# A one-core diffusion step: Pool's low parts of weight blocks in pieces of 256 columns

## The chip, the cores and the metric

The program runs on one core of one Trainium2 chip. The metric is the device time of one execution in microseconds (us). The engines are named as in the profile: PE (matrix products), PEld (its weight loads, which overlap), DVE (VectorE), ACT (ScalarE), POOL (GpSimd) and SP (SyncE, which here issues the DMAs). A row with SPq is SP's queue.

## The reference

Two layers of a hybrid backbone in fp32, with shared weights for 128 context tokens and 1024 latent tokens, D_MODEL = 1024, D_FF = 2816:

```python
def layer(x, cond, w, ctx=None):
    ...
    mods = jax.nn.silu(cond) @ w_ada + b_ada
    ...
    h = rms_norm(x, g_pre_mix) * (1 + sc_m) + sh_m
    q_na, k_na, v_na, q_mla, ckv, k_rope, q_g, k_g, v_g = mixer_projections(
        h, w_in, mla_g_q, mla_w_uq, mla_g_kv, gqa_g_q, gqa_g_k)
    ...
    o = jnp.concatenate([o_na, o_mla, o_gqa], axis=-1) @ w_out
    x = x + gt_m * rms_norm(o, g_post_mix)
    h = rms_norm(x, g_pre_ffn) * (1 + sc_f) + sh_f
    x = x + gt_f * rms_norm(conv_ffn(h, ffn_w_up, ffn_conv_w, ffn_conv_b, ffn_w_down), g_post_ffn)
```

The three attentions are a neighbourhood attention, a multi-head latent attention and a grouped-query attention. `conv_ffn` is an up-projection, a convolution of width 3 over the tokens, a SiLU gate and a down-projection.

## The kernel before

The nine token tiles (128 tokens each, the context tile first) go through both layers together. A layer has five phases. The first is the projections with `w_in` (phase A), in layer 0 with the modulation's matrix `w_ada` among them. Then come the attentions. The output projection with `w_out` (phase C, `phase_c`) makes eight products of 1024 columns for each token tile, block k of the weights being row k of `w_out`; each tile ends with two RMS norms. The up-projection (`phase_u`) takes 44 blocks of `w_up` a layer, each with 72 matmuls of 384 columns (eight rows, three products, three groups of tokens), and DVE runs the convolution (L1020) behind them. The down-projection takes 66 loads of `w_down` a layer, in three groups of three token tiles, and ends each group with the norms of its tiles.

A matmul in fp32 is made of three products of rounded operands: high times high, high times low, low times high. So every operand is split. `load_w` (L341 to L350) brings 512 KB by one DMA of SP into one of two raw buffers (`wraw`, L348), and `split` (L194 to L200) makes two tiles from it: ACT copies the raw values into the rounded high part (L197), and Pool or DVE subtracts the high part from the raw one, which gives the low part (L200). Who subtracts is set by `lo_eng`: Pool for all of `w_up`; Pool and DVE in turn for `w_in`, `w_out` (even k on Pool, odd k on DVE) and `w_down`. The next DMA into a raw buffer waits until both parts were made from it. SP issues its DMAs in the order of the program, so what stands behind such a DMA waits with it: in the up-projection that is also `wadv` (L305), a piece of `w_ada` for `ada_dve`, in which DVE adds products of that piece into `aacc` (L308, L311) and PE then transposes the sums (L320).

In phase C DVE has one row of work at the start: the low parts of the nine tiles of `Y` (the attentions' output, last written at L734), named `hlo<-Y`, and of the odd weight blocks. The names of the weights' tiles there are `wu` for k = 0 and 1, `wd` for 2 and 3, `wx` for 4 to 7, so that the loads of the first four use the room of the FFN's weights. The products are in L973: for the first three token tiles k = 0 to 3 first, then the tiles one by one with the rest.

The norms run as `norm_tiles`: L166 multiplies the products in PSUM by the gain (`wt`), which frees PSUM for PE; `rsqrt_newton` makes 1/sqrt of a column in some six instructions of one column each (L116, L120, tiles `nw_t` and `nw_u`); L175 adds into the residual (`xt`). Each engine runs its instructions in the order in which the program issues them; the generators of several tiles are advanced in turn, so that one tile's Newton steps can stand ahead of another's L166 in DVE's row. The down-projection's products are L1125; the operand `g` is split like the weights.

Only blocks held as three-dimensional tiles are `weights` of 1024, 832 or 768 columns (a tile's two middle axes multiplied); those of 512 columns and two-dimensional tiles are split by the same function.

Of the kernel before, what the change touches and what calls it, by code (L numbers as in the profile page):

```python
# [14 lines left out]
F32 = mybir.dt.float32  # L15
# [4 lines left out]
ALU = mybir.AluOpType  # L20
# [25 lines left out]
def tile_kernel(ctx: ExitStack, tc: tile.TileContext, I, O):  # L46
    nc = tc.nc
    act, dve, pool, pe = nc.scalar, nc.vector, nc.gpsimd, nc.tensor
# [146 lines left out]
    def split(raw, hi, lo, hi_eng=None, lo_eng=None):  # L195
        if hi_eng is None:
            act.copy(hi, raw)  # L197
        else:
            hi_eng.tensor_copy(hi, raw)
        (lo_eng or pool).tensor_tensor(out=lo, in0=raw, in1=hi.bitcast(F32), op=ALU.subtract)  # L200

    def evac2(hi, lo, src, scale=None):

# [138 lines left out]
    def load_w(wp, src, tag, bufs, lo_eng=pool, wr=None):  # L342

        na, nb = src.shape[1:]
        raw = (wr or wp).tile([128, 1024], F32, name="wraw", bufs=2)
        out = [wp.tile([128, 1024], F32R, name=f"{tag}{i}", bufs=bufs) for i in range(2)]
        raw, hi, lo = [t.rearrange("p (a b) -> p a b", a=na)[:, :, :nb] for t in (raw, *out)]
        nc.sync.dma_start(out=raw, in_=src)  # L348
        split(raw, hi, lo, lo_eng=lo_eng)
        return hi, lo  # L350
# [12 lines left out]
    def phase_a(l, z, H, w, before, rest):  # L363
# [47 lines left out]
        ukv = [ml.tile([128, 512], F32R, name=f"ukv{i}", bufs=1) for i in range(2)]  # L411
        ckvT = [ml.tile([128, NT + 128], F32R, name=f"ckvT{i}", bufs=1) for i in range(2)]
        split(uq_r, uq[0], uq[1])
        split(ukv_r, ukv[0], ukv[1])
        split(cc_r, ckvT[0][:, 128:256], ckvT[1][:, 128:256])

# [809 lines left out]
    for l in range(L):  # L1226
# [49 lines left out]
        gens, xs, owner = [], {}, {}  # L1276
# [146 lines left out]
```

## Time and profile before

| | |
|---|---|
| time, median of 3 runs | 3352.62 us (3351.02 to 3357.26) |
| the profiled execution's own time | 3349.35 us |
| its span in the trace | 3347.5 us |
| PE busy | 3193.8 us, 95% of the span |
| DVE busy | 2164.2 us, 65% |
| ACT busy | 1545.5 us, 46% |
| POOL busy | 1127.4 us, 34%, 962 instructions |
| granted clock of PE, mean | 0.988 of full speed |

The profiled execution is one of many; its own time is measured around the program, the span is what the trace holds of it. Durations in the rows below come from that one execution. The busy share is an average: how much an engine's time is worth is read from the places where PE is idle. In the rows, the text in square brackets is the idle time of the engine just before the instruction, and what ended it.

### The profile page before, as it was taken

How to read it: one execution, taken by the hardware profiler on the slowest of the kernel's cores; microseconds unless marked ns; L12 is line 12 of the kernel's file. 1: busy time of each engine (PE TensorE's matmuls, PEld its weight loads, DVE VectorE, ACT ScalarE, POOL GpSimd, SP SyncE). 2: the span in 40 equal slices, each digit the busy share in tenths (PEclk: the TensorE clock that was granted, in tenths of full speed). 3: DMA queues.
4: the chain of work that ended last, by engine and by line, in shares of the span. 5: the costliest groups of instructions: out<-in, count | busy, mean ns of one | idle time of the engine just before them, and what ended most of it. 6: DMA issues, size and time to landing. Idle time of an engine off the chain costs nothing.

```text
span 3347.5 us, 50944 instructions
## 1 busy us (share of the span) xinstructions
PE 3193.8 (95%) x18068; PEld 2883.7 (86%) x18068; DVE 2164.2 (65%) x5367; ACT 1545.5 (46%) x3209; POOL 1127.4 (34%) x962
## 2 busy tenths in 40 slices
PE   8988999989999999999999899999899999999999
PEld 3868888877899999987788799888779999999887
DVE  5796788887787888435547728888768433333443
ACT  4321688885322222235544228888743222223443
POOL 2122345431233323344421314554313322323443
PEclk9999999999999999999999999999999999999999
DMA  7467431254244333255644563215523221213665
GB/s 244 137 180 225 138 78 46 62 158 144 85 142 127 118 120 118 79 186 192 194 139 135 152 194 84 54 46 128 167 87 107 88 73 60 73 66 122 205 205 167
DMA packets 224863, 428.77 MB, mean 128 GB/s; under 512 B 21089, under 2 KB 127457, under 8 KB 224609
## 3 DMA queue, kind: packets, MB, share of 16 engines
q1 hardware_dynamic: 223312, 424.33, 41.3%
q8 instruction: 143, 2.34, 0.3%
q10 hardware_dynamic: 1296, 1.19, 0.1%
q14 instruction: 112, 0.91, 0.1%
HBM read 324.05 MB, written 101.38 MB: 127 GB/s over the span
## 4 chain that ended last, share of the span: by engine, by line
PE 70%; DVE 14%; ACT 6%; issue 4%; DMA 3%; POOL 2%; SPq 1%; ACTq 0%; DVEq 0%; POOLq 0%
PE mm L1008 31%; PE mm L1125 15%; PE O L727 4%; PE T L709 4%; PE SA L679 3%; PE mm L973 3%; ACT P L689 2%; PE mm L591 2%; DVE PT L206 2%; ACT PT L205 2%; DVE aacc L311 2%; PE mm L376 1%; PE mm L375 1%; PE mm L374 1%; DVE nw_t L116 1%
## 5 line engine op out<-in xcount | busy, mean ns | idle before, releaser
L1008 PE MATMUL mm<-hhi,wu 128*128 128x384 f32 x4224 | 863.2, 335 | 2.4 <-POOL wu L200 1.5
L1008 PEld LDWEIGHTS mm<-hhi,wu 128*128 128x128 f32 x4224 | 742.6, 188 | 3.7 <-POOL wu L200 2.2
L1020 DVE SCALAR_TENSOR_TENSOR acc<-mm,conv,acc 128x336 f32<-128x336 f32 (+6 forms) x1408 | 412.6, 374 | 312.7 <-ACT acc L1045 312.5
L200 POOL TENSOR_TENSOR wu<-wraw,wu 128x1024 fp32r<-128x1024 f32 x123 | 301.9, 2456 | 688.5 <-ACT wu L197 673.8
L1008 PE MATMUL mm<-hlo,wu 128*128 128x384 f32 x2112 | 490.8, 334 | 0.0
L197 ACT CAST wu<-wraw 128x1024 fp32r<-128x1024 f32 x158 | 165.7, 1050 | 598.4 <-issue 371.8
L1008 PEld LDWEIGHTS mm<-hlo,wu 128*128 128x128 f32 x2112 | 377.1, 188 | 0.6 <-DVE hlo L153 0.4
L698 POOL TENSOR_SCALAR P<-P,rs 128x1152 f32<-128x1152 f32 (+3 forms) x288 | 273.3, 949 | 192.5 <-DVE rs L697 143.1
L727 PE MATMUL O<-PT,V 128*128 128x256 f32 (+1 forms) x1936 | 321.0, 295 | 10.8 <-DVE Y L734 10.8
L311 DVE SCALAR_TENSOR_TENSOR aacc<-wadv,sc,aacc 128x512 f32<-128x512 f32 x280 | 261.2, 976 | 65.6 <-DMA wadv<-w_ada 65.1
L709 PE MATMUL T<-ident,P 128*128 128x128 f32 x1736 | 282.4, 278 | 16.7 <-DVE PT L206 10.5
L679 PE MATMUL SA<-k,q 128*128 128x256 f32 (+5 forms) x1224 | 281.5, 350 | 11.5 <-DVE mx L818 3.8
L1125 PE MATMUL mm<-wd,g 128*128 128x512 f32 x1224 | 286.7, 390 | 2.6 <-DVE wt L166 2.6
L206 DVE TENSOR_TENSOR PT<-T,PT 128x512 fp32r<-128x512 f32 (+1 forms) x424 | 270.8, 646 | 22.2 <-ACT PT L205 16.7
L727 PEld LDWEIGHTS O<-PT,V 128*128 128x128 f32 x1936 | 258.3, 190 | 20.3 <-DVE Y L734 16.3
L1125 PE MATMUL mm<-wu,g 128*128 128x512 f32 x1152 | 272.1, 392 | 2.6 <-DVE wt L166 2.6
L1125 PEld LDWEIGHTS mm<-wd,g 128*128 128x128 f32 x1224 | 229.1, 188 | 51.0 <-DVE wt L166 3.5
L1125 PEld LDWEIGHTS mm<-wu,g 128*128 128x128 f32 x1152 | 217.2, 189 | 48.7 <-DVE wt L166 3.5
L205 ACT CAST PT<-T 128x512 fp32r<-128x512 f32 (+1 forms) x424 | 231.0, 561 | 53.3 <-PE T L709 39.0
L709 PEld LDWEIGHTS T<-ident,P 128*128 128x128 f32 x1736 | 199.6, 141 | 50.2 <-DVE PT L206 15.7
L679 PEld LDWEIGHTS SA<-k,q 128*128 128x128 f32 (+1 forms) x1224 | 197.9, 192 | 35.5 <-ACT P L689 7.2
L702 DVE TENSOR_REDUCE mx<-SA 128x1 f32<-128x896 f32 (+1 forms) x192 | 182.2, 949 | 33.2 <-PE SA L679 32.9
(207 smaller groups left out, 5083.0 us busy)
## 6 DMA issues: line engine op xcount, KB each, us to landing
wraw<-w_down SPq DMA_DIRECT2D x132, 512.0 KB, 3.6
wraw<-w_up SPq DMA_DIRECT2D x88, 512.0 KB, 3.6
wadv<-w_ada SPq DMA_DIRECT2D x160, 256.0 KB, 2.9
GT<-acc SPq DMA_DIRECT2D x44, 576.0 KB, 2.8
graw<-GT SPq DMA_DIRECT2D x132, 192.0 KB, 3.1
k<-KT SPq DMA_DIRECT2D x64, 320.0 KB, 5.9
q<-QT SPq DMA_DIRECT2D x48, 288.0 KB, 5.7
XD<-xt SPq DMA_DIRECT2D x27, 512.0 KB, 3.0
```

The costliest lines, as they stand in the source:

```text
L200: (lo_eng or pool).tensor_tensor(out=lo, in0=raw, in1=hi.bitcast(F32), op=ALU.subtract)
L205: act.copy(hi, src)
L206: dve.tensor_tensor(out=lo, in0=src, in1=hi.bitcast(F32), op=ALU.subtract)
L311: dve.scalar_tensor_tensor(out=accs[i], in0=w, scalar=sc[:, k, i:i + 1], in1=accs[i], op0=ALU.mult, op1=ALU.add)
L679: pe.matmul(out, q[0:rows, qc:qc + 128], kview(k[0:rows]), start=(i == 0), stop=(i == len(passes) - 1))
L698: pool.tensor_scalar(out=P[:, :n], in0=P[:, :n], scalar1=rs, scalar2=1.0, op0=ALU.mult, op1=ALU.mult)
L702: dve.tensor_reduce(out=out, in_=src, op=ALU.max, axis=AX.X, negate=True)
L709: pe.transpose(tp[:, j * 128:(j + 1) * 128], p, ident)
L727: pe.matmul(op[0][:, c0:c1], V[:, vt, :], PT[e][:, sl, c0:c1], start=(i == 0 and e == 0), stop=(i == last and e == 1))
L1008: pe.matmul(pts[c][:, :CN], a[:, k, :], h_[:, k, c * CN:(c + 1) * CN], start=(k == 0 and a is whi and h_ is hhi), stop=(k == KC - 1 and a ...
L1020: dve.scalar_tensor_tensor(out=d, in0=src, scalar=w, in1=d, op0=ALU.mult, op1=ALU.add)
L1125: pe.matmul(pts[j], a[:, ts], d[:, 0, j * 512:(j + 1) * 512], start=(f == 0 and n == 0), stop=(f == NFF - 1 and n == 2))
```

## The change

Pool's subtraction of a low part is cut into four instructions along the columns where the block is a three-dimensional tile of more than 512 columns. A block with eight rows of 128 columns (`w_up`, `w_down`) is cut into pairs of rows; one with a single row of 1024 (`w_out`) into four quarters of it; one with two rows (`w_in`, and the query's up-projection) into halves of each row. A piece has 256 columns (208 for the four blocks of 832, 192 for the two of 768). DVE's subtractions and ACT's copies stay whole.

```diff
-        (lo_eng or pool).tensor_tensor(out=lo, in0=raw, in1=hi.bitcast(F32), op=ALU.subtract)
+        for lo, raw, hi in quarters(lo, raw, hi) if lo_eng is None or lo_eng is pool else [(lo, raw, hi)]:
+            (lo_eng or pool).tensor_tensor(out=lo, in0=raw, in1=hi.bitcast(F32), op=ALU.subtract)
+
+    def quarters(*xs):
+
+        if len(xs[0].shape) != 3 or xs[0].shape[1] * xs[0].shape[2] <= 512:
+            return [xs]
+        na, nb = xs[0].shape[1:]
+        if na == 8:
+            return [[x[:, i:i + 2] for x in xs] for i in range(0, 8, 2)]
+        h = nb * na // 4
+        return [[x[:, a:a + 1, c:c + h] for x in xs] for a in range(na) for c in range(0, nb, h)]
```

It touches 178 blocks: 123 with the name `wu`, 37 `wd`, 4 `wx`, 12 `w` and 2 `uq`. They were 178 instructions and are now 712; nothing else is added, and no instruction passes another on any engine. In the program after, L200 stands at L201 and later lines 11 further down.

On Pool, at the start of phase C in layer 0, the row before (wu, wd, wx, wx are the low parts of blocks 0, 2, 4 and 6 of `w_out`):

```order
L698 TENSOR_SCALAR P<-P,rs 128x384 [waits DVE_49,PE_49]
L200 TENSOR_TENSOR wu_9418<-wraw,wu_9417 128x1024 [waits DMAHW4_49,DMAHW3_49,DMAHW5_49,DMAHW2_49,DMAHW6_49,DMAHW1_49,DMAHW7_49,DMAHW0_49,Activation_49]
L200 TENSOR_TENSOR wd_9434<-wraw,wd_9433 128x1024 [waits DMAHW4_49,Activation_49]
L200 TENSOR_TENSOR wx_9450<-wraw,wx_9449 128x1024 [waits DMAHW6_49,DMAHW7_49,DMAHW0_49,Activation_49]
L200 TENSOR_TENSOR wx_9466<-wraw,wx_9465 128x1024 [waits DMAHW1_49,DMAHW3_49,DMAHW0_49,DMAHW5_49,PE_49,Activation_49]
```

And the same place after:

```order
L709 TENSOR_SCALAR P<-P,rs 128x384 [waits DVE_49,PE_49]
L201 TENSOR_TENSOR wu_9439<-wraw,wu_9438 128x256 [waits DMAHW4_49,DMAHW3_49,DMAHW5_49,DMAHW2_49,DMAHW6_49,DMAHW1_49,DMAHW7_49,DMAHW0_49,Activation_49]
L201 TENSOR_TENSOR wu_9439<-wraw,wu_9438 128x256 x3
L201 TENSOR_TENSOR wd_9458<-wraw,wd_9457 128x256 [waits DMAHW4_49,Activation_49]
L201 TENSOR_TENSOR wd_9458<-wraw,wd_9457 128x256 x3
L201 TENSOR_TENSOR wx_9477<-wraw,wx_9476 128x256 [waits DMAHW6_49,DMAHW7_49,DMAHW0_49,Activation_49]
L201 TENSOR_TENSOR wx_9477<-wraw,wx_9476 128x256 x3
L201 TENSOR_TENSOR wx_9496<-wraw,wx_9495 128x256 [waits DMAHW1_49,DMAHW3_49,DMAHW0_49,DMAHW5_49,PE_49,Activation_49]
L201 TENSOR_TENSOR wx_9496<-wraw,wx_9495 128x256 x3
```

Every block stands where it stood, as four pieces, and the first piece has the waits of the whole one. The DMAs into the raw buffers on SP still wait for Pool's last piece.

On PE, in a block of the up-projection in layer 0 (wu_11027 and wu_11028 are the block's high and low part), the row before:

```order
L1008 MATMUL mm<-hhi,wu_11028 128x384 [waits Pool_49]
L1008 MATMUL mm<-hhi,wu_11028 128x384 x2
L1008 MATMUL mm<-hhi,wu_11027 128x384 x3
L1008 MATMUL mm<-hlo,wu_11027 128x384 x3
L1008 MATMUL mm<-hhi,wu_11028 128x384 x3
L1008 MATMUL mm<-hhi,wu_11027 128x384 x3
L1008 MATMUL mm<-hlo,wu_11027 128x384 x3
L1008 MATMUL mm<-hhi,wu_11028 128x384 x3
```

And after (wu_11072 and wu_11073 are the same two parts):

```order
L1019 MATMUL mm<-hhi,wu_11073 128x384 [waits Pool_49]
L1019 MATMUL mm<-hhi,wu_11073 128x384 x2
L1019 MATMUL mm<-hhi,wu_11072 128x384 x3
L1019 MATMUL mm<-hlo,wu_11072 128x384 x3
L1019 MATMUL mm<-hhi,wu_11073 128x384 x3
L1019 MATMUL mm<-hhi,wu_11072 128x384 x3
L1019 MATMUL mm<-hlo,wu_11072 128x384 x3
L1019 MATMUL mm<-hhi,wu_11073 128x384 [waits Pool_49]
L1019 MATMUL mm<-hhi,wu_11073 128x384 x2
```

Before, PE waited for Pool once a block; after, it waits again at every second of the eight rows, where the next piece begins.

## Rows read from the trace of the kernel before

**Rows 1.** The page's busy time, share of the span, instructions.

```profile
PE 3193.8 (95%) x18068; PEld 2883.7 (86%) x18068; DVE 2164.2 (65%) x5367; ACT 1545.5 (46%) x3209; POOL 1127.4 (34%) x962
```

**Rows 2.** Chain of waits, 1035 to 1080: start us, us, what.

```profile
1037.57 37.45 PE mm L1008 x216
```

**Rows 3.** Instructions of L200: duration ns min/median/max, first and last start us.

```profile
L200 POOL TENSOR_TENSOR wu<-wraw,wu x123: 2364/2405/3044, 740.8 to 3312.5; 128x1024 fp32r<-128x1024 f32 x123
L200 POOL TENSOR_TENSOR PT<-rt,PT x80: 727/735/746, 364.2 to 2296.6; 128x256 fp32r<-128x256 f32 x80
...
L200 DVE TENSOR_TENSOR hlo<-Y,hhi x18: 1209/1218/3365, 745.9 to 2406.1; 128x1024 fp32r<-128x1024 f32 x18
```

**Rows 4.** Instructions of L116, the Newton step.

```profile
L116 DVE SCALAR_TENSOR_TENSOR nw_t<-nw_u,nw_v x192: 203/219/2401, 6.7 to 3342.7; 128x1 f32<-128x1 f32 x192
```

**Rows 5.** Timeline, 847 to 912: start us, us, engine line operation.

```profile
847.70 4.75 POOL L200 TENSOR_TENSOR wu<-wraw,wu 128x1024 fp32r<-128x1024 f32 x2 [8.90 <-ACT wu L197]
847.72 2.40 DVE L116 SCALAR_TENSOR_TENSOR nw_t<-nw_u,nw_v 128x1 f32<-128x1 f32 x1
...
858.59 0.69 PE L148 MATMUL aux<-ident,wt 128*128 128x128 f32 x2 [5.64 <-ACT wt L188]
...
909.02 2.84 POOL L200 TENSOR_TENSOR wu<-wraw,wu 128x1024 fp32r<-128x1024 f32 x1
```

**Rows 6.** Timeline, down-projection of layer 1, then of layer 0.

```profile
3157.92 2.73 POOL L200 TENSOR_TENSOR wd<-wraw,wd 128x1024 fp32r<-128x1024 f32 x1 [7.78 <-ACT wd L197]
3158.32 2.35 DVE L116 SCALAR_TENSOR_TENSOR nw_t<-nw_u,nw_v 128x1 f32<-128x1 f32 x1
3161.33 1.89 PE L1125 MATMUL mm<-wu,g 128*128 128x512 f32 x7 [1.31 <-DVE wt L166]
...
1541.27 2.37 POOL L200 TENSOR_TENSOR wd<-wraw,wd 128x1024 fp32r<-128x1024 f32 x1 [2.73 <-ACT wd L197]
1541.63 2.42 DVE L200 TENSOR_TENSOR g<-graw,g 128x384 fp32r<-128x384 f32 x1 [2.63 <-ACT g L197]
1546.36 1.12 PE L148 MATMUL aux<-ident,wt 128*128 128x128 f32 x4 [3.94 <-DVE ht L152]
```

**Rows 7.** Timeline, DVE in the projections of layers 0 and 1.

```profile
107.83 2.47 DVE L311 SCALAR_TENSOR_TENSOR aacc<-wadv,sc,aacc 128x512 f32<-128x512 f32 x1
...
1903.46 1.47 DVE L487 TENSOR_SCALAR nw_v<-nw_v 128x8 f32<-128x8 f32 x1
```

**Rows 8.** Timeline, start of phase C in layer 0, by engine.

```profile
742.12 2.15 DVE L200 TENSOR_TENSOR wu<-wraw,wu 128x1024 fp32r<-128x1024 f32 x1 [0.53 <-ACT wu L197]
745.89 3.50 DVE L200 TENSOR_TENSOR hlo<-Y,hhi 128x1024 fp32r<-128x1024 f32 x3 [1.17 <-ACT hhi L197]
753.80 7.97 DVE L200 TENSOR_TENSOR hlo<-Y,hhi 128x1024 fp32r<-128x1024 f32 x5
...
748.78 2.88 POOL L200 TENSOR_TENSOR wd<-wraw,wd 128x1024 fp32r<-128x1024 f32 x1 [5.58 <-ACT wd L197]
756.40 3.15 POOL L200 TENSOR_TENSOR wx<-wraw,wx 128x1024 fp32r<-128x1024 f32 x1 [4.75 <-ACT wx L197]
...
759.58 0.33 SPq L348 DMA_DIRECT2D wraw<-w_out  x1
762.97 1.05 ACT L197 CAST wx<-wraw 128x1024 fp32r<-128x1024 f32 x1 [3.78 <-DMA wraw<-w_out]
767.01 1.07 PE L973 MATMUL mm<-wx,hhi 128*128 128x512 f32 x4
```

**Rows 9.** Timeline, start of the up-projection in layer 0.

```profile
892.27 4.92 POOL L200 TENSOR_TENSOR wu<-wraw,wu 128x1024 fp32r<-128x1024 f32 x2 [3.72 <-ACT wu L197]
897.64 0.38 SPq L305 DMA_DIRECT2D wadv<-w_ada  x1
921.03 0.66 PE L320 MATMUL aux<-ident,aacc 128*128 128x128 f32 x4 [1.76 <-DVE aacc L311]
```

## The prediction

> **What bounds the kernel now.** I read the page's busy shares first, then the longest pieces of the chain of waits, then durations by line, then the timeline of each place where TensorE (PE) stands idle. PE is busy for 95% of the span and Pool for 34% [rows 1]. In the up-projection 216 matmuls, three blocks of 72, run through in 37.45 us, 173 ns for each, with no piece of another engine in between; they already hold three satisfied waits for Pool [rows 2]. So Pool's speed is worth nothing there. What Pool can do to the time sits where PE starves: at the ends of tile groups, at the start of the output projection, at the start of the up-projection, in the projections. These rows I read for who stands behind a Pool block.
>
> Two facts carry the rest. First, a DVE instruction with two operands in SBUF does not run beside a Pool block: the Newton step nw_t takes 219 ns in the median and 2401 ns at most, which is the length of a Pool block [rows 3, 4], and at 847.72 it lasts 2.40 us, exactly beside the Pool row of 847.70 [rows 5]. The Trainium skill has this as a rule ("SBUF — State Buffer", § Who interferes with whom): the shared port pair is an exclusive lock, held for the whole instruction. The trace agrees (2401 against 219). By that rule alone a quarter of the instruction is a quarter of the wait; that outcome is the first rival below.
> Second, it goes both ways and the two engines take turns: the Pool block that starts at 909.02 while DVE adds up takes 2.84 us, where the median is 2.405 [rows 3, 5], and the Pool blocks at 748.78 and 756.40, beside DVE's row of low parts, take 2.88 and 3.15 [rows 8]. Today Pool pays that once a block. In four pieces it can pay it at each.
>
> **The change part by part.** No instruction moves past another; 178 Pool instructions become 712.
>
> *Pool's own time.* A block of 1024 columns costs 2405 ns, a piece of 256 columns 735 ns [rows 3], the same operation on the same types: 4 x 735 = 2940, +0.535 a block, at most 178 x 0.535 = 95 us of Pool's time. Starts overlap by about 0.06, so I count 0.675 a piece, 2.7 a block. Pool's 1127 us of 3347 [rows 1] hide it: PE in the up-projection, where 88 blocks stand, has its low parts long before. Without that cover it would be 0.3 to 0.5 for each block that PE waits for.
>
> *New waits on PE and DMA.* PE now waits for Pool four times in a block of the up-projection (264 more waits). Each is for something long done; the three blocks of 37.45 us with their three such waits show no gap [rows 2], so 0. (Were a satisfied wait to cost 10 ns, an estimate from nothing finer than the 173 ns a matmul, it would be 2.6 us in all; I keep that for the range.) Pool's later pieces wait for nothing, and the DMA into the raw buffer still waits for the last piece.
>
> *Ends of groups in the down-projection, layer 1.* At 3157.92 a Pool block starts; nw_t behind it takes 2.35 us, the tile wt that frees PE's PSUM stands behind nw_t, and PE idles 1.31 before 3161.33 [rows 6]. With pieces, nw_t goes in after at most 0.68, wt starts some 1.4 us earlier and the gap closes. There are two such gaps in layer 1: 2 x -1.31 = **-2.6**. The bounds are 0 and -2.6.
>
> *The same in layer 0.* Two like gaps close, but each is followed by an older wait that swallows the gain: PE idles 3.94 before 1546.36 for the transposed tile [rows 6]. That chain itself stands behind a Pool block: 1541.27, with DVE's g taking 2.42 beside it [rows 6] where a free one, at the rate of a 1024-column DVE split of 1.22 [rows 3], would take about half a microsecond. After: g goes in after one piece, then a piece, then DVE's weights between two more. I count 1.0 to 1.15 saved at each of two ends: **-2.2**. Bounds: 0, and twice 2.42 - 0.5 = 1.9, that is -3.8.
>
> *Projections.* Eleven DVE instructions on PE's way are drawn out by a Pool block; the first at 107.83 takes 2.47, the last at 1903.46 takes 1.47 [rows 7]. For a lone one the wait falls from a block to a piece, 2.47 - 0.74 - 0.68 = 1.05. In a chain it doesn't: one block over a Newton chain of six costs 2.40 + 5 x 0.22 = 3.5 now; in pieces four of the six wait one piece, 4 x 0.68 + 2 x 0.22 = 3.2, saving 0.3. Most of the eleven have another such instruction right behind, so 0.3 each: **-3.3**. Bounds 0 and 11 x 1.05 = -11.6.
>
> *End of the output projection.* Two blocks (4.75) stand over one Newton chain at 847.70, whose end releases PE after 5.64 idle at 858.59 [rows 5]. Eight pieces over the six instructions of the chain: 6 x (0.68 + 0.2) = 5.3 against 4.75 + 4 x 0.22 = 5.6. I take 0.4 a layer: **-0.8**; bounds 0 and -1.
>
> *Start of the output projection.* Here it goes against the change. DVE's weight split at 742.12 takes 2.15 beside a Pool block [rows 8]; with pieces it is done 1.0 sooner, and PE starts this stage 1.0 sooner. But then DVE runs a dense row of two-operand splits (three take 3.50 from 745.89 when free, 1.1 each in a row; five take 7.97 from 753.80), and Pool makes the low parts of blocks 2 and 4 in the midst of it [rows 8]. Block 2: four pieces and up to three DVE splits between them, 2.7 + 2 to 3 x 1.1, ends about 754.2 instead of 748.78 + 2.88 = 751.66. The DMA of block 4 waits for that, so its copy ends near 758.6 instead of 756.3, and its pieces take turns with DVE until DVE's row is out near 762.9; the last ends about 763.7 instead of 759.55, +4.1. Block 6's DMA is issued at 759.58, right after block 4's low part, and its copy runs from 762.97 [rows 8]: it would be done at 768.1 instead of 764.02. PE wants it at 767.01 - 1.0 = 766.0 [rows 8]; the 3.0 us of slack is gone. Then come block 6's own pieces, 2.7, and some 0.3 for DVE's block 7: low parts complete at 771.1, where PE read the second half of them by about 767.7. Net **+3.4 a layer, +6.8**. Low end: pieces aren't stretched, and PE keeps its 1.0: -2.0 for both. High end: a whole DVE split at every piece, also of block 6 (3 x 1.1 more): +6.6 a layer, +13.
>
> *Start of the up-projection.* Two blocks at 892.27 end at 897.19 [rows 9]. Four DVE additions for the modulation now go in between the pieces, and the last ends about 899.3. SP's next raw-buffer DMA waits for that, and the load wadv that DVE needs stands behind it in SP's queue (issue 897.64 [rows 9]), so it lands 2.1 later. At 909.02 about 1.0 comes back, as DVE no longer waits for a whole block. PE restarts at 921.03 when the addition is done [rows 9]: +1.2 a layer (what PE gains ahead of it only makes that wait longer), **+2.4**. Bounds: -2.0 (1.0 regained, nothing lost) and +4.2.
>
> The sum is -2.6 - 2.2 - 3.3 - 0.8 + 6.8 + 2.4 = +0.3. It is made against the profiled execution, 3349.35 us (a span of 3347.5 and 1.85 around it); that gives 3349.7. The median of the runs shown lies 3.27 above the profiled one, so 3353.
>
> **The rivals.**
> *Waits shrink, nothing stretches (faster).* If DVE gets in between pieces and Pool's pieces hardly wait, the losses fall away: -2.6 - 2.2 - 3.3 - 0.8, -2.0 from the earlier start of the output projection, 0 at the up-projection: -10.9, about 3342. For it: the gaps of 1.31 stand right behind a block. Against it: 2.84 and 3.15 for blocks beside DVE [rows 5, 8].
> *Output projection starves (slower).* The place is block 4 among DVE's splits; the price is up to 6.6 a layer; it decides once block 4's last piece ends later than 759.55 + 3.0 - 1.0 = 761.6, from where each us later is one of PE's. With +13 there, +2.4, and half the gains of the projections and groups (-4.5) it is +11, about 3363; with +10 there it is 3360. For it: DVE is dense there. Against it: once DVE's row is out, pieces run free.
> *All covered.* PE is at 95% and its gaps have other causes; -2 to +2, 3350 to 3355.
>
> **How the numbers follow.** The median can tell about 0.2%, 6.7 us, from no change: faster is under 3345.9, slower over 3359.3. Chances: the forecast 0.45, all covered 0.10, faster rival 0.25, slower rival 0.20. Of the forecast 0.02 spill over to slower. So faster 0.25, same 0.53, slower 0.22. The range takes in the faster rival at 3342 and the slower one up to 3361; the likeliest case's own is 3347 to 3358.
>
> **What would show it.** Pool pieces of about 0.67 to 0.74 and 712 of them; in layer 1 no gap for wt at the two ends of groups; nw_t at most near 0.9; block 4's last piece at the output projection 3 to 5 us later after that stage's start than before, and a new wait of PE for block 6, 2 to 5 us; wadv landing later at the start of the up-projection; 216 matmuls still in 37.45. The forecast is wrong if PE finds no new wait in the output projection (then the faster rival), if that wait is over 6 us a layer, or if matmuls in the up-projection take longer than 173 ns with their new waits.

## The result and the profile after

The changed kernel is slower, by half a percent: 3368.68 us in the median (3367.43 to 3374.83, 6 runs) against 3351.86 (3350.49 to 3361.0, 6 runs) of the kernel before on the same chips; the ratio is 1.0052, 95% interval 1.0041 to 1.0063. The forecast was 3353 with a range of 3342 to 3361. The profiled execution took 3367.43, its span is 3365.6, 18.1 longer than the one before.

The page's first line, which answers to [rows 1]:

```profile
PE 3210.3 (95%) x18068; PEld 2894.3 (86%) x18068; DVE 2121.5 (63%) x5367; ACT 1543.9 (46%) x3209; POOL 1247.1 (37%) x1496
```

Pool is busy 120 us longer and DVE 43 us shorter. PE, which does the same matmuls, is busy 16.5 us longer and idle 155.3 us instead of 153.7 (span less busy time). So the waits that are new and the old ones that closed nearly cancel, and most of the 18.1 us is matmuls that ran slower; the granted clock is 0.983 in the mean, where it was 0.988. The durations of L201 and of the Newton step answer to [rows 3, 4]:

```profile
L201 POOL TENSOR_TENSOR wu<-wraw,wu x492: 719/739/1782, 737.3 to 3332.8; 128x256 fp32r<-128x256 f32 x164
...
L116 DVE SCALAR_TENSOR_TENSOR nw_t<-nw_u,nw_v x192: 202/220/933, 6.8 to 3360.9; 128x1 f32<-128x1 f32 x192
```

The change does what it says: a piece takes 739 ns, and nw_t at most 933 where it took 2401. But a piece now takes up to 1782, more than twice its median.

Where the 18.1 us arose is read from the start of the same matmul in the two traces:

| the same PE instruction | before | after | later by |
|---|---|---|---|
| first product of the output projection, layer 0 | 745.91 | 742.14 | -3.8 |
| in its second part | 801.76 | 805.17 | +3.4 |
| in the up-projection, first block | 922.37 | 926.16 | +3.8 |
| in the last group of the down-projection | 1658.87 | 1662.62 | +3.8 |
| projections of layer 1, transposes of cn | 1783.07 | 1790.01 | +6.9 |
| first product of the output projection, layer 1 | 2391.49 | 2396.71 | +5.2 |
| in its second part | 2447.30 | 2458.02 | +10.7 |
| second product of the down-projection | 3067.33 | 3078.70 | +11.4 |
| its last group | 3299.98 | 3318.16 | +18.2 |

So three places lose: the output projection (+7.2 and +5.5), the projections of layer 1 (+3.7 at one wait), and the down-projection of layer 1 (+6.8). The rest is small. In both output projections and in the down-projection of layer 1, PE is idle longer and also busy longer. The stretches from the first to the second matmul of the table in each stage, before and after (columns: stretch, its length, then busy us and count of PE, PEld, DVE, ACT, POOL, granted clock, DMA share, GB/s), are

```profile
745.91:801.76 55.85, 54.87 (x240) 43.37 (x241) 43.92 (x100) 32.41 (x61) 12.45 (x10) 0.96 0.51 181
2391.49:2447.30 55.81, 54.66 (x239) 43.09 (x240) 43.98 (x100) 32.39 (x61) 12.49 (x10) 0.97 0.50 181
3067.33:3299.98 232.65, 230.02 (x1014) 189.83 (x1012) 92.21 (x144) 94.47 (x140) 103.00 (x57) 1.00 0.64 208
```
```profile
742.14:805.17 63.03, 58.65 (x240) 45.45 (x240) 43.07 (x100) 32.58 (x61) 16.39 (x19) 0.91 0.46 167
2396.71:2458.02 61.31, 58.43 (x239) 44.75 (x240) 42.96 (x100) 32.56 (x61) 16.38 (x19) 0.92 0.46 171
3078.70:3318.16 239.46, 233.71 (x1013) 191.15 (x1012) 88.42 (x144) 93.37 (x140) 122.15 (x141) 0.99 0.61 202
```

Of the 7.2, 5.5 and 6.8 us that they lose, 3.4, 1.7 and 3.1 are idle time, and 3.8, 3.8 and 3.7 are the same matmuls taking longer. The up-projection, with half of all cut blocks, is as it was: the row of the chain of waits that answers to [rows 2] is

```profile
2578.31 37.45 PE mm L1019 x216
```

*Output projection, layer 0*, timeline, answering to [rows 8]:

```profile
742.14 1.22 PE L984 MATMUL mm<-wu,hhi 128*128 128x512 f32 x2 [2.45 <-ACT hhi L197]
...
745.74 4.79 POOL L201 TENSOR_TENSOR wd<-wraw,wd 128x256 fp32r<-128x256 f32 x4 [4.66 <-ACT wd L197]
756.55 4.80 POOL L201 TENSOR_TENSOR wx<-wraw,wx 128x256 fp32r<-128x256 f32 x4 [6.03 <-DMA wraw<-w_out]
759.64 1.72 POOL L201 TENSOR_TENSOR wx<-wraw,wx 128x256 fp32r<-128x256 f32 x1
765.99 2.78 POOL L201 TENSOR_TENSOR wx<-wraw,wx 128x256 fp32r<-128x256 f32 x4 [4.64 <-ACT wx L197]
...
757.45 3.31 DVE L201 TENSOR_TENSOR hlo<-Y,hhi 128x1024 fp32r<-128x1024 f32 x2 [3.58 <-ACT hhi L197]
760.68 1.75 DVE L201 TENSOR_TENSOR wx<-wraw,wx 128x1024 fp32r<-128x1024 f32 x1
...
764.87 1.04 ACT L197 CAST wx<-wraw 128x1024 fp32r<-128x1024 f32 x1 [5.55 <-DMA wraw<-w_out]
...
765.97 0.74 PE L984 MATMUL mm<-wx,hhi 128*128 128x512 f32 x2 [2.12 <-ACT wx L197]
767.47 0.57 PE L984 MATMUL mm<-wx,hhi 128*128 128x512 f32 x1 [0.76 <-POOL wx L201]
768.83 0.80 PE L984 MATMUL mm<-wx,hhi 128*128 128x512 f32 x1 [0.79 <-POOL wx L201]
```

Blocks 2 and 4 take 4.8 on Pool (2.88 and 3.15 before): two of the four pieces each last nearly as long as a piece and a DVE split together (the row of 759.64 is the last piece of block 4 by itself), and DVE's splits beside them take 1.75 instead of 1.22. Block 6's pieces run free, 2.78 for four. Block 4 is done 19.2 after the stage's first product; it was 13.6. The copy of block 6 ends at 765.91, and PE, 2.12 idle, starts on it at 765.97. Then it waits twice more, for the pieces of block 6 themselves. What follows is slow: the windows 766 to 776, of before and of after, are

```profile
766.00:776.00 10.00, 10.00 (x45) 8.03 (x44) 5.52 (x15) 4.01 (x10) 0.48 (x1) 1.00 0.95 372
```
```profile
766.00:776.00 10.00, 8.45 (x23) 5.91 (x24) 3.60 (x10) 2.31 (x5) 2.78 (x4) 0.66 1.01 407
```

After the idle times the granted clock is 0.66 in the mean, that is the lower of its two levels (1.2 GHz) for most of the stretch, and PE gets through 23 matmuls instead of 45. In layer 1 the waits for block 6 are shorter, 0.45, 0.76 and 0.87, and the clock falls behind them too (0.72 from 2422 to 2428); there about 1.0 of the loss lies at the stage's start already, where the clock stays low longer than before.

*Down-projection, layer 1.* The first end of a group went as forecast: no gap for wt where [rows 6] had 1.31 (28 matmuls run through from 3168.73). At the second, PE waits four times for wt:

```profile
3168.73 6.57 PE L1136 MATMUL mm<-wu,g 128*128 128x512 f32 x28
...
3260.63 2.40 PE L1136 MATMUL mm<-wd,g 128*128 128x512 f32 x7 [1.69 <-DVE wt L166]
3264.37 1.43 PE L1136 MATMUL mm<-wd,g 128*128 128x512 f32 x5 [1.34 <-DVE wt L166]
3266.28 0.80 PE L1136 MATMUL mm<-wd,g 128*128 128x512 f32 x1 [0.49 <-DVE wt L166]
3268.89 7.28 PE L1136 MATMUL mm<-wd,g 128*128 128x512 f32 x22 [1.80 <-DVE wt L166]
```

The name of the wait is the same, but another thing stands behind it. The chain of waits of the stage, with the 45 us ahead of them:

```profile
3078.64 134.80 PE mm L1136 x594
...
3217.54 3.46 DMA wraw<-w_down
3222.23 2.82 POOL wd L201 x4
3225.07 3.44 DMA wraw<-w_down
...
3240.16 5.07 DMA wraw<-w_down
3246.47 3.80 POOL wu L201 x4
...
3258.69 1.28 DVE wd L201
3259.97 1.20 DVE wt L166 x2
```

Here the end is set by a loop: a load, its copy, Pool's pieces, the next load into the same raw buffer. A lap takes 7.5 (3217.54 to 3225.07), for two loads, since the other buffer runs beside it; PE uses two loads up in 36 x 134.80 / 594 = 8.2. So the loads gain 0.6 a lap on PE; in the kernel before a lap at this place takes 7.2 (issues at 3216.89 and 3224.05), which gains 1.0. And after a group's end the laps are longer. The times at which SP issues every second load, before and after:

```profile
3170.04 0.40 SPq L348 DMA_DIRECT2D wraw<-w_down  x1
...
3177.93 0.33 SPq L348 DMA_DIRECT2D wraw<-w_down  x1
...
3186.06 0.33 SPq L348 DMA_DIRECT2D wraw<-w_down  x1
...
3194.69 0.33 SPq L348 DMA_DIRECT2D wraw<-w_down  x1
```
```profile
3182.30 0.34 SPq L359 DMA_DIRECT2D wraw<-w_down  x1
...
3191.65 0.33 SPq L359 DMA_DIRECT2D wraw<-w_down  x1
...
3200.21 0.33 SPq L359 DMA_DIRECT2D wraw<-w_down  x1
...
3209.72 0.33 SPq L359 DMA_DIRECT2D wraw<-w_down  x1
```

Three laps took 24.7 and now take 27.4. Turns have a share in that: the Pool block at this end lasts 4.23 (from 3169.30), where it lasted 2.73 [rows 6]. The kernel before had its lead back by the second group's end: there ACT waits for PE to free a tile. In the kernel after it still waits for the load (first row before, second after):

```profile
3235.78 0.52 ACT L197 CAST g<-graw 128x384 fp32r<-128x384 f32 x1 [2.57 <-PE mm L1125]
```
```profile
3236.17 1.05 ACT L197 CAST wd<-wraw 128x1024 fp32r<-128x1024 f32 x1 [2.98 <-DMA wraw<-w_down]
```

The last lap is the longest, 10.1 (3240.16 to an issue at 3250.30), with a load of 5.07 and a block drawn out to 3.80; why that load was slow stays open. So at the group's end DVE's split of a late load (3258.69 in the chain) stands right in front of the tiles wt that free PE's PSUM.

*Projections of layer 1*: Pool's block of 832 columns, before and after, and PE's wait that follows:

```profile
1770.63 1.99 POOL L200 TENSOR_TENSOR w<-wraw,w 128x832 fp32r<-128x832 f32 x1 [4.45 <-ACT w L197]
```
```profile
1776.20 3.22 POOL L201 TENSOR_TENSOR w<-wraw,w 128x208 fp32r<-128x208 f32 x4 [5.83 <-ACT w L197]
...
1790.01 0.90 PE L457 MATMUL aux<-ident,cn 128*128 128x128 f32 x3 [3.86 <-DVE cn L441]
```

The loads of `w_uq` wait for this block in the same way. The block of 832 columns just before it takes 3.2 instead of 1.99 as well.

### The profile page after: what moved, and what is told of

It is laid out like the page before. It is cut to its first block, busy times and chain, and to the rows that moved or that the text cites. A ratio compares the mean times of both kernels' runs of the same rounds, so it can differ in the third digit from the quotient of the medians.

```text
span 3365.6 us, 51581 instructions
## 1 busy us (share of the span) xinstructions
PE 3210.3 (95%) x18068; PEld 2894.3 (86%) x18068; DVE 2121.5 (63%) x5367; ACT 1543.9 (46%) x3209; POOL 1247.1 (37%) x1496
## 5 line engine op out<-in xcount | busy, mean ns | idle before, releaser
L201 POOL TENSOR_TENSOR wu<-wraw,wu 128x256 fp32r<-128x256 f32 x492 | 382.3, 809 | 662.1 <-ACT wu L197 620.3
L322 DVE SCALAR_TENSOR_TENSOR aacc<-wadv,sc,aacc 128x512 f32<-128x512 f32 x280 | 242.2, 907 | 79.7 <-DMA wadv<-w_ada 79.3
L738 PEld LDWEIGHTS O<-PT,V 128*128 128x128 f32 x1936 | 259.5, 191 | 19.5 <-DVE Y L745 15.5
```

The costliest lines, as they stand in the source:

```text
L322: dve.scalar_tensor_tensor(out=accs[i], in0=w, scalar=sc[:, k, i:i + 1], in1=accs[i], op0=ALU.mult, op1=ALU.add)
L738: pe.matmul(op[0][:, c0:c1], V[:, vt, :], PT[e][:, sl, c0:c1], start=(i == 0 and e == 0), stop=(i == last and e == 1))
```

## The experiments

Each is timed against the kernel before on its own chip; a ratio stands with its 95% interval. The theory after the result: a cut block keeps its raw buffer longer (0.4 by itself, up to 2 where DVE gets in between), and where the loads have little lead that is PE's time. The rivals are that each piece or each new wait costs something wherever it is, and that it is DVE's steps that come late.

**One stage at a time.** `only_a`, `only_c`, `only_u`, `only_d` cut only the blocks of one stage:

```diff
-        for lo, raw, hi in quarters(lo, raw, hi) if lo_eng is None or lo_eng is pool else [(lo, raw, hi)]:
+        for lo, raw, hi in quarters(lo, raw, hi) if (lo_eng is None or lo_eng is pool) and cut in CUT else [(lo, raw, hi)]:
+    CUT = ('A',)                     # only_a: w_in, uq
+    CUT = ('C0', 'C2', 'C4', 'C6')   # only_c: w_out, block by block
+    CUT = ('U',)                     # only_u: w_up
+    CUT = ('D',)                     # only_d: w_down
```

> Cut only in the projections' blocks (w_in, uq). Theory (raw-buffer loop: a cut Pool block ends later, and so does the next load into its raw buffer): +4 to +7 us, nearly all at the start of layer 1's projections, where TensorE then waits some 3.9 us for cn. Rival (the loss comes from waits on TensorE or from all pieces alike, so in proportion to blocks): 18 of 178 blocks here, +1 to +2 us. Rival (what I had predicted, drawn-out DVE steps get shorter): -3 us.

Measured: 1.0003 (0.9994 to 1.0012), -2 to +4 us. Inconclusive in time: the interval just reaches the theory's least, +4. The wait is there in its trace, and its Pool blocks of 832 columns take 3.2 as in the kernel after:

```profile
1787.58 0.59 PE L459 MATMUL aux<-ident,cn 128*128 128x128 f32 x3 [3.78 <-DVE cn L443]
```

> Cut only in the eight w_out blocks that Pool splits (four a layer). Theory (raw-buffer loop plus taking turns with DVE): the stage starts 2 to 4 us earlier and then waits for blocks 4 and 6, net +5 to +8 us for both layers. Rival (in proportion to blocks, 8 of 178): under +1 us.

Measured: 1.0045 (1.0032 to 1.0058), +15 us, nearly twice the most that was expected. Eight of 178 blocks cost nearly as much as all; block 4 takes 4.80 and PE waits 2.45 for block 6. In proportion to blocks it would have been under 1.

> Cut only in the 88 w_up blocks, 264 new waits on TensorE. Theory (loads have slack here): -2 to +2 us, and 216 matmuls still in 37.45 us. Rival (each new wait or each piece costs TensorE something): half of all cut blocks are here, so +8 us.

Measured: 1.0001 (0.9992 to 1.0010). 216 matmuls still take 37.45. With 88 cut blocks and 264 new waits, the rival that each piece or wait costs PE something falls.

> Cut only in the 66 w_down blocks that Pool splits. Theory (raw-buffer loop; loads fall behind after a group's end and have not caught up by the next): +5 to +8 us, at the second end of a group in layer 1. Rival (in proportion to blocks, 66 of 178): +6 us, but spread over both layers. Rival (my prediction): -4.8 us.

Measured: 1.0018 (1.0009 to 1.0027), +6 us. In its trace the loss lies at the second group's end of layer 1, with the waits

```profile
PE mm L1138 <- DVE wt L166: 5.6, 4, 1.9
```

(in total, times, longest) as in the kernel after. The four runs add up to about +22, where all cuts together cost 17; each of them is uncertain by 3 to 4.

**The raw buffers of the down-projection.** A third one, for every third load; `all_d3` has it with all blocks cut, `none_d3` with none, `d_d3` with those of `w_down` alone:

```diff
-        raw = (wr or wp).tile([128, 1024], F32, name="wraw", bufs=2)
+        raw = (wr or wp).tile([128, 1024], F32, name="wraw", bufs=1 if wr is not None and cut == "D" else 2)
...
-            wd = load_w(self.wp, I["w_down"][self.l, f], ("wd", "wu")[i // 2 % 2], 2, e)
+            wd = load_w(self.wp, I["w_down"][self.l, f], ("wd", "wu")[i // 2 % 2], 2, e, wr=self.gp if i % 3 == 2 else None, cut="D")
```

> The changed kernel, with every third load of w_down going to a raw buffer of its own, so that the loop of the down-projection has three raw buffers and not two. Theory (the longer Pool block holds the raw buffer, loads lose their lead over TensorE): the waits at the second group's end in layer 1 go and the time falls by 5 to 9 us against the changed kernel, to 3359 to 3364. Rival (DVE's steps at the group's end are late because Pool's pieces come between them): no change, 3368.

Measured: 3357.6 us, 1.0022 (1.0013 to 1.0031), where the kernel after has 1.0052. It is 10 us faster than that one (through the kernel before, on different chips), a little more than expected: layer 0 gains as well, its down-projection is 3.9 shorter than before in the trace.

> The kernel before, with the same third raw buffer in the down-projection and whole blocks: the control. Theory: its loads have their lead already when a group ends, and its gaps are for wt behind a Pool block, so -2 to +1 us against before. Were it -5 or more, the third buffer would be a gain of its own and say nothing on the cut.

Measured: 1.0006 (0.9997 to 1.0015). The control: without the cut the third buffer gives nothing (+2, where at most +1 was expected), and the two old waits stay:

```profile
PE mm L1138 <- DVE wt L166: 2.6, 2, 1.3
```

> Cut only in w_down, with the third raw buffer there; everything else as before. Theory (the gain of the faster version is that of the ends of groups): -6 to -2 us against before, where the same cut with two raw buffers cost +7. Rival (the gain came from w_up and block 0 of w_out): -1 to +1 us.

Measured: 0.9983 (0.9974 to 0.9992), -6 us. The same cut cost +6 with two raw buffers and gives 6 with three. From 3228 to 3262, the stretch with the second group's end, PE doesn't stand still for a moment, and the clock stays up; `only_d` in its like stretch stands behind it:

```profile
3228.00:3262.00 34.00, 34.00 (x151) 28.14 (x150) 21.98 (x44) 15.55 (x28) 17.72 (x20) 1.00 0.54 175
```
```profile
3234.00:3268.00 34.00, 28.25 (x108) 21.21 (x107) 18.99 (x43) 14.84 (x27) 15.74 (x18) 0.90 0.55 168
```

That settles the down-projection: what is lost there is lost by the raw buffer, and what is left is the gain that was forecast. In this trace the down-projections of layers 0 and 1 are 3.7 and 3.2 shorter than before; the forecast had 2.2 and 2.6.

**Longer, or oftener interrupted?** `all_half` cuts in two, `all_tail` makes the block whole and its last 128 columns once more:

```diff
-            return [[x[:, i:i + 2] for x in xs] for i in range(0, 8, 2)]
-        h = nb * na // 4
+            return [[x[:, i:i + 4] for x in xs] for i in range(0, 8, 4)]   # all_half
+        h = nb * na // 2
+        return [xs, [x[:, na - 1:na, nb - 128:nb] for x in xs]]            # all_tail, instead of both
```

> All blocks in two pieces of 512 columns (416, 384 for the small ones). Pool's own time for a block is near 2.5, 0.1 over the whole block; DVE gets in once. Theory of turns: +3 to +8 us over before, block 4 of the output projection about 3.6 to 4.2. Theory of Pool's own time: a quarter of the loss, +4 us. The two meet here in total, the length of block 4 tells them apart (2.5 to 3.2 by Pool's own time, as before).

Measured: 1.0002 (0.9994 to 1.0011), +1 us; the theory's least, +3, is just within the interval. Block 4 takes 3.53, near its 3.6, so DVE did get in. The trace shows two parts that offset each other: the output projections are 3.6 and 1.3 longer than before, the down-projections 1.5 and 2.1 shorter.

> Instead of the cut, each of the 178 blocks is made whole and then its last 128 columns once more (0.47 us): Pool is busy as long as with four pieces (2.8 against 2.75), but DVE can get in once and not three times. Theory of turns (what costs is that DVE gets in between pieces): a third to a half of the loss, +4 to +8 us over before; block 4 of the output projection in layer 0 takes 3.6 to 4.7 where four pieces take 4.8. Theory of Pool's own time (0.4 more in each block): the whole loss, +15 to +18 us.

Measured: 1.0075 (1.0063 to 1.0088), +25 us. Both theories missed. Block 4 takes 3.81, as by turns, and in the output projections little is lost, 1.6 and 1.4 in the trace. The down-projections lose 1.8 and 8.7; there it may have both faults, as the whole block still holds DVE and the loop is longer. The rest lies between the output and the down-projection (3.3 and 4.0) and in the projections of layer 1 (3.5). The block 4 of both, and PE's wait at the first end of a group in layer 0 with the tail (1.3 before):

```profile
758.11 3.53 POOL L201 TENSOR_TENSOR wx<-wraw,wx 128x512 fp32r<-128x512 f32 x2 [6.10 <-DMA wraw<-w_out]
```
```profile
758.71 3.81 POOL L201 TENSOR_TENSOR wx<-wraw,wx 128x1024 fp32r<-128x1024 f32 x2 [4.80 <-DMA wraw<-w_out]
...
1533.33 3.90 PE L1134 MATMUL mm<-wu,g 128*128 128x512 f32 x10 [3.16 <-DVE wt L166]
```

So there are two mechanisms with one outcome. In the output projection it is the turns, three of them in four pieces. In the down-projection the two runs point to Pool's own time: each gives DVE one place to get in, and the one that adds 0.1 to a block gains there, the one that adds 0.5 loses. They differ in where that place lies too, and the kernel after has turns there as well, so the shares aren't shown apart.

**Which blocks of w_out.** `c06` cuts only blocks 0 and 6 (`CUT = ('C0', 'C6')`), not the two that stand beside DVE's row.

> Cut only in blocks 0 and 6 of w_out, two a layer; blocks 2 and 4, beside DVE's row of low parts, stay whole. Theory of turns: the loss of the kernel with all four cut (14 us) goes, block 4 takes 3.1 as in the kernel before, TensorE finds block 6 in time, and the stage starts 0.9 us sooner for block 0: -3 to 0 us against before. Rival (any cut block of w_out costs the same): half the loss, +7 us.

Measured: 1.0000 (0.9992 to 1.0009). Block 4, whole, takes 3.17, and PE finds block 6 in time; its only wait there is 0.28, for a block that DVE splits:

```profile
756.08 3.17 POOL L201 TENSOR_TENSOR wx<-wraw,wx 128x1024 fp32r<-128x1024 f32 x1 [4.72 <-ACT wx L197]
```

Since cutting blocks 2 and 4 as well costs 15 (`only_c`), it is these four blocks of 178 that bring the loss; they weren't cut alone.

**A version that beats both.** `best_d3` cuts block 0 of w_out, w_up and w_down, with the third raw buffer; `best_half` cuts the same in halves, with two:

```diff
+    CUT = ('C0', 'U', 'D')
```

> Cut in block 0 of w_out, in w_up and in w_down, with the third raw buffer for w_down; w_in, uq and blocks 2, 4, 6 of w_out whole. Theory: the waits for wt at the ends of groups go (-2.6 in layer 1, up to -2 in layer 0), the output projection starts up to 1 us sooner in each layer, nothing is lost: -7 to -3 us against before. Rival (pieces always cost more than they give): +1 to +7 us.

Measured: 3344.99 us, 0.9982 (0.9973 to 0.9991), -6 us. `d_d3` is not told from it, so no gain from w_up or block 0 is shown.

> The same choice of blocks in halves of 512 columns, and two raw buffers. Theory: a half holds DVE for 1.25 and Pool loses one turn at most, so most of the waits for wt go without the loads falling behind: -5 to -1 us against before. Rival (without the third buffer the cut in w_down costs what it costs in quarters): +5 to +8 us.

Measured: 0.9996 (0.9987 to 1.0006), not told from before, with -5 to -1 expected. The waits for wt in layer 1 did shrink, from 1.31 to 0.2 at each end, and in the trace the down-projections are 1.7 and 2.2 shorter than before with two raw buffers; the time doesn't show it.

## Why the prediction was wrong

The step that failed is "Pool's own time": I put the longer block at nothing, with "Pool's 1127 us of 3347 [rows 1] hide it", and named only PE in the up-projection as the one who might miss it. I did write that the DMA into the raw buffer still waits for the last piece, and followed that wait in the output projection and at the start of the up-projection, but not through the down-projection and the projections. A share of busy time says nothing of a loop with two buffers. Its size was off too: "at most" 95 us became 120. Alone, a block costs 2.82 instead of 2.405, which makes 74 for 178 blocks; the rest, an estimate of some 45, is turns.

A second thing is missing in the whole sum: what a wait of PE does to its clock. In the two output projections and the down-projection of layer 1, 11 of the 19.5 us lost are slower matmuls. Of the signs that the prediction named for itself, the second gap for wt alone failed outright; block 4's last piece came 5.6 later after the stage's start, where 3 to 5 were named.

- *Ends of groups, layer 1* (-2.6 forecast): +6.8. The gap of the first end closed, and PE is 1.5 less late behind it. At the second, the loads had not caught up. With a third raw buffer no wait is left in that stage, so the forecast's mechanism was right and its cover missing.
- *The same in layer 0* (-2.2): 0 by the table at 1658.87, and -0.6 when the next stage begins (1781.45 is now 1784.66); with the third buffer the trace of `d_d3` has that stage 3.7 shorter.
- *Projections* (-3.3): +4.1 in layer 1 (3.2 late at 1781.45, 7.3 at 1924.30). The drawn-out DVE steps did get shorter, but the block of 832 columns went from 1.99 to 3.22 and the loads behind it came late. By the time of `only_a` alone this isn't settled. In layer 0, PE is 1.4 earlier at 273.90, but 1.1 later in `only_a` with the same cut there, so a gain isn't shown either.
- *Start of the output projection* (+3.4 a layer from a start 1.0 sooner, so 4.4 of loss): the mechanism and the place were right. The wait of PE for the copy (2.1 forecast) was 2.12 in layer 0, but 0.45 in layer 1. When the last wait for block 6 in layer 0 is over, PE has lost 4.9, near the 4.4; the loss of the stage was 7.2, and 5.5 in layer 1. What was mis-sized is what follows the waits: I had no term for the clock, which fell to 0.66 there.
- *End of the output projection* (-0.8 for both layers): -0.5 in each, -1.1 in both; in layer 0 the gap of [rows 5] went from 5.64 to 5.11, over eight pieces in 6.03:

```profile
851.10 6.03 POOL L201 TENSOR_TENSOR wu<-wraw,wu 128x256 fp32r<-128x256 f32 x8 [8.91 <-ACT wu L197]
...
861.45 0.69 PE L148 MATMUL aux<-ident,wt 128*128 128x128 f32 x2 [5.11 <-ACT wt L188]
```

- *Start of the up-projection* (+2.4): +2.1 for both layers, 0.9 and 1.2. As forecast, `wadv` is issued later, at 902.75 instead of 897.64, of which 2.9 is the stage itself; the wait of [rows 9] is 1.86 instead of 1.76, and PE waits twice more ahead of it, 0.47 and 0.66, for DVE's convolution.
- *New waits on PE*: 0, as forecast.

The slower rival named the right place and its 13 us were near the 12.7 measured there, but that is luck in part: it had a DVE split at every piece of block 6 too, which ran free, and no term for the clock. Against its loss it set half of the gains, which the same longer block took away elsewhere; and its own sum, 3363, lay outside the range that was to take it in. The attention, where nothing is cut, is 2 to 3 us shorter in the trace after than in that of before; other traces here show differences of that kind there too, and what they are stays open. The first row of the table holds it.

## What to carry to other kernels

A small instruction holds another engine for less time, but the work takes longer in all, and where another engine's instructions are held up by it and hold it up in turn, as DVE's here, each cut is one more place for the other to get in. Before cutting, look for who waits for the last piece: if it is the next load into one of two buffers, the block is part of a loop, and that loop's lap against the consumer's pace decides, not the engine's busy share. Count a short wait of PE at more than its length: here the slower matmuls behind such waits cost as much again. Cut with a further buffer, or only where the loads have lead.

## What the runs showed of the hardware

A Pool piece of 256 columns (739 ns in the median) and a DVE split of 1024 columns (1.22 alone) that contend take turns: in the output projection each lasts nearly as long as both, 1.72 the piece and 1.75 the split. In `all_tail` the further 128 columns make a block 2.92 where DVE is quiet (block 6) and 3.81 where it is not (block 4), for an instruction of 0.47 alone.

Behind an idle time of 2.12 us with two short ones (0.76 and 0.79) PE had a granted clock of 0.66 in the mean over 10 us, and behind three of 0.45, 0.76 and 0.87 one of 0.72 over 6 us. One wait of 1.31 by itself, in the kernel before at 3252.70, left it at 1.00 (3248 to 3258). In the output projection of layer 0 the slower matmuls cost 3.8 us, for 3.4 us more of idle time.
